# Up projections with 512-column matmuls over both operand parts, and new prices in the planner of an encoder kernel

## The chip, the core and the metric

One NeuronCore of a Trainium2 chip runs the whole program. TensorE (PE) multiplies, VectorE (DVE) and ScalarE (ACT) do the elementwise work, GpSimd (POOL) issues a few copies, SyncE (SP) issues nearly all loads. The metric is the device time of one execution in microseconds.

## What is computed

Two layers on x of 256 frames by 1024 channels, all in float32. Cut to what matters here:

```python
def swiglu_ffn(x, w_up, w_down):              # w_up: 1024 x 5632, w_down: 2816 x 1024
    a, b = jnp.split(x @ w_up, 2, axis=-1)
    return (jax.nn.silu(a) * b) @ w_down

for l in range(DEPTH):                        # DEPTH = 2
    x = x + 0.5 * swiglu_ffn(rmsnorm(x, ffn1_norm[l]), ffn1_w_up[l], ffn1_w_down[l])
    proj = rmsnorm(x, mix_norm[l]) @ w_in[l]  # 1024 x 5120
    # three branches on parts of proj: S5 state space model, chunked attention,
    # convolution module; each gated, summed, then one projection w_out
    x = x + merged @ w_out[l]
    x = x + 0.5 * swiglu_ffn(rmsnorm(x, ffn2_norm[l]), ffn2_w_up[l], ffn2_w_down[l])
```

## The kernel before

Activations are held transposed: 128 channels on the partitions, 256 frames along the free axis. So a weight tile is 128 x 128, stationary, and 256 columns of frames pass over it. To keep nearly float32 accuracy with the faster F32R matmul, each operand is split in two parts, `hi` and `lo` = value - `hi`, and a product is hi x hi + hi x lo + lo x hi.

Weights come from HBM in chunks of eight tiles (512 KB). For each chunk SP loads `raw` (3 buffers), ACT casts it to `hi` (4 buffers), DVE subtracts to get `lo` (4 buffers). A few small branch weights stay in float32 and are loaded straight into `lo` buffers. A norm's two parts of the operand lie side by side in one tile `x2` (128 x 8 x 2 x 256), in the profile `x`; the gated FFN activations lie the same way in a tile `a2`, in the profile `AB`.

`ffn` (four calls) has an up stage and a down stage. The up stage runs over 22 pairs of column blocks: block `i` gives the part through the silu, block `22 + i` the factor. Each block is 8 tiles, three matmuls of 256 columns each in `prod` (operands given as a tuple). Both halves of a pair share one PSUM bank of 512 columns, taken in turn from the rings `mm` (3 banks) and `at` (2). Then DVE multiplies the first half by `rb` (the norm's factor, spread over the partitions), ACT takes a tanh, DVE finishes the silu and multiplies by the second half from PSUM, ACT and DVE split the result into `AB`. The scratch tiles of this are the ring `ev` (4 buffers). The down stage runs over 8 column blocks of 22 tiles; `prod` gets its operand as one tile there, and passes both parts at once over a `hi` tile (512 columns, the hi x hi sum in the left half of the bank, hi x lo in the right) and the `hi` part over the `lo` tile (256 columns, left half). ACT copies the right half out, DVE adds the left.

The other PSUM rings are `pq`, `y` (S5 branch) and `ax` (norms, attention outputs, convolution norm), one bank each. A norm's end (`norm_end`) sums squares with four matmuls of one column (`ax<-ones,acc`), takes a reciprocal root on DVE, and spreads it by a slow float32 matmul (`ax<-sq,ones`) that ACT copies to `rb`. The convolution's layer norm in the mixer (`conv_norm`) ends in the same way: DVE makes `sq`, PE spreads it, ACT copies, DVE multiplies `cv` with it and goes on, and then `cv` feeds the branch matmuls `w_br_conv`. The `gh` tile of the S5 branch feeds `s5_w_glu` beside them.

The program is not written in the order in which it runs. A recorder takes every operation; `schedule` then plays a list scheduling with a price for each (`price`: how long it holds its engine, and the delay until its result counts), and the instructions are issued in the order found, each engine in order. Among ready operations the lowest rank goes first: -2 for a norm's end, 0 for the main line, 1 for the attention heads, 2 for the convolution, 3 for the S5 states, 4 for the S5 tables of a layer (given to `ffn1` as `fill`, made on DVE and ACT from scratch tiles `sa`, `sc`, `mc`, `bs` for use in that layer's mixer). All helper matmuls of ranks over 0 run as -1. Since every recorded operation is issued from one line, all have one line in the profile (L289); they are told apart by tiles.

Of the kernel before, what the change touches and what calls it, by code (L numbers as in the profile page):

```python
# [18 lines left out]
F32R = mybir.dt.float32r  # L19
I32 = mybir.dt.int32  # L20
AF = mybir.ActivationFunctionType
ALU = mybir.AluOpType
AX = mybir.AxisListType
PSUM = bass.MemoryType.PSUM

L, P, T, DM, DFF = 2, 128, 256, 1024, 2816
KD, KF = DM // P, DFF // P
# [99 lines left out]
class Recorder:  # L127
# [85 lines left out]
    @staticmethod  # L213
    def price(eng, name, outs, ins, kw):
        n = 1
        for d in list(outs[0].ap)[1:]:
            n *= d[1]
        if name == "dma_start":
            return (max(0.5, 1.43e-3 * n), 2.0) if eng == "sp" else (1.0, 2.0 + 2.5e-3 * n)
        if eng == "pe":  # L220
            if name == "transpose":
                return 0.112, 0.2
            slow = kw["rhs"].dtype != F32R or n < 256
            rows = outs[0].partition_size()
            return max(n / 2400.0 * (4 * rows / P if slow else 1) + 0.0025, 0.03), 0.2
        if eng == "act":
            return 0.12 + n / 1200.0 + (0.1 if kw.get("accum_out") is not None else 0), 0.2
        if name == "reciprocal":
            return 0.06 + 8 * n / 960.0, 0.16
        if name == "tensor_reduce":  # L230
            n = 1
            for d in list(ins[0].ap)[1:]:
                n *= d[1]
        fast = name in ("tensor_scalar", "tensor_copy") and all(a.space != PSUM for a in outs + ins)
        scal = 0.06 if any(a.free_size() == 1 for a in ins) and n > 1 else 0
        return SLACK * (0.068 + scal + n / (1920.0 if fast else 960.0)), 0.16

    def schedule(self):
        import heapq
# [52 lines left out]

X_LOADS = {(0, 0): (0, 1), (0, 512): (1, 2), (1, 0): (2, 4), (2, 0): (4, 8)}
MARGIN, AUX_MARGIN = 0.3, 0.8
SLACK = 1.02
WARM = 5
RAW = 3
RANKS = (1, 2, 3)
# [2 lines left out]
class Builder:  # L301
# [183 lines left out]
    def ffn(self, l, name, after=None, fill=()):  # L485
        nc = self.nc
        up, down = name + "_w_up", name + "_w_down"
        a2 = self.tile(self.big, [P, KF, 2, T], F32R, "AB")
        fill = list(fill)
        first = l == 0 and name == "ffn1"  # L490
        ops = (self.xh, self.xl)
        pq = []
        for i in range(KF):
            if i == 0 and first:
                pq = [self.bank(t)[:, :T] for t in ("mm", "mm", "mm", "at")]
                self.quad(pq, l, up, (0, KF, 1, KF + 1), ops, KD)
                self.norm_end()
            elif i == 0:
                pq = [self.bank()[:, :T] for _ in range(2)]
                self.pair(pq, l, up, (0, KF), ops, KD)  # L500
                self.norm_end()
            elif not pq:
                ps = self.bank(("mm", "mm", "mm", "at", "at")[(i + 1) % 5])
                pq = [ps[:, :T], ps[:, T:]]
                for o, c in zip(pq, (i, KF + i)):
                    self.block(o, l, up, c, ops, KD)
            rb = self.rb
            t = self.tmp("ev")
            nc.vector.tensor_tensor(out=t, in0=pq.pop(0), in1=rb, op=ALU.mult)
            th = self.tmp("th")  # L510
            nc.scalar.activation(out=th, in_=t, func=AF.Tanh, scale=0.5)
            nc.vector.scalar_tensor_tensor(out=t, in0=th, scalar=1.0, in1=t, op0=ALU.add, op1=ALU.mult)
            nc.vector.tensor_tensor(out=t, in0=t, in1=pq.pop(0), op=ALU.mult)
            nc.scalar.copy(out=a2[:, i, 0, :], in_=t)
            nc.vector.tensor_tensor(out=a2[:, i, 1, :], in0=t, in1=a2[:, i, 0, :].bitcast(F32), op=ALU.subtract)
            if i == 0:
                self.rank(4)
                for f in fill:
                    f()
                self.rank(0)  # L520
        if after is not None:
            self.norm_start(*after)

        def evac(j, ps):
            t = self.tmp("ev")
            nc.scalar.copy(out=t, in_=ps[:, T:])
            nc.vector.tensor_tensor(out=t, in0=ps[:, :T], in1=t, op=ALU.add)
            nc.vector.scalar_tensor_tensor(out=t, in0=t, scalar=0.25, in1=rb, op0=ALU.mult, op1=ALU.mult)
            nc.vector.tensor_tensor(out=self.x[:, j, :], in0=self.x[:, j, :], in1=t, op=ALU.add)
            if after is not None:  # L530
                self.norm_block(j)
            else:
                nc.sync.dma_start(out=self.out_d[:, j, :], in_=self.x[:, j, :])

        p2 = [self.bank(), self.bank()]
        self.pair(p2, l, down, (0, 1), a2, KF)
        for j in range(KD):
            ps = p2[j] if j < 2 else self.bank()
            if j >= 2:
                self.block(ps, l, down, j, a2, KF)  # L540
            evac(j, ps)
# [584 lines left out]
```

## Time and profile before

| | us |
|---|---|
| median of 3 runs (1165.84 to 1168.61) | 1166.5 |
| the profiled execution | 1166.6 |
| its span, first to last instruction | 1164.8 |
| PE matmul busy in it | 1151.6 |
| DVE busy | 924.8 |
| ACT busy | 643.9 |

The span is what the trace covers; the execution's own time is 1.8 us more. The stages can be found by what PE reads: `x` in the up stages and `w_in`, `AB` in the down stages, `cv`, `u` and `gh` in the branch projections, `tbl` in `w_out`. In the order of time: up stage 4.7 to 136.7 us, down stage to 198.9, mixer of layer 0 to 397.5, up to 525.0, down to 586.9, then layer 1 in the same way from 586.9. "Idle before" is the time that an engine stood still ahead of an instruction, with what ended it. A matmul's duration (0.28 us for 256 columns) holds its way through the array; the next one starts after some 0.12, so pitches are read from starts.

### The profile page before, as it was taken

Reading aid. Unit: us, or ns where it says so; the run is one execution under the profiler, and the core shown is the slowest. Engines: PE = TensorE matmul, PEld = TensorE weight load, DVE = VectorE, ACT = ScalarE, POOL = GpSimd, SP = SyncE. Lnnn points to the kernel's source line nnn. Section 1 sums busy time; section 2 is a strip of 40 time slices with the busy share of each in tenths; the row PEclk is TensorE's granted clock in tenths of the full one; section 3 lists DMA queues with packets and bytes.
Section 4 is the critical chain, followed back from the end, with each engine's and each line's share of the span. In section 5 each row is a group of like instructions: output and inputs, shape, how many; then the busy total and the mean of one; then the engine's idle time right before and its main releaser. Section 6 shows DMA issues by size and latency. Waiting matters only on the chain.

```text
span 1164.8 us, 21936 instructions
## 1 busy us (share of the span) xinstructions
PE 1151.6 (99%) x8565; PEld 1086.8 (93%) x8565; DVE 924.8 (79%) x1898; ACT 643.9 (55%) x1171; POOL 13.0 (1%) x32
## 2 busy tenths in 40 slices
PE   8999999999998999999999999999999999999998
PEld 7999988889997999998899999898999999999987
DVE  7999976899998888766676666769999897666654
ACT  7546654797662556544544444547876535444442
POOL 0000000000200000000000000000001000000000
PEclk9999999999999999999999999999999999999999
DMA  7655556654542665555555555566554436555562
GB/s 258 216 182 182 191 184 217 199 194 152 172 153 93 182 198 181 192 184 186 184 178 184 184 187 188 183 217 200 180 166 157 145 125 191 187 184 183 181 200 89
DMA packets 59751, 209.97 MB, mean 180 GB/s; under 512 B 6912, under 2 KB 9088, under 8 KB 59392
## 3 DMA queue, kind: packets, MB, share of 16 engines
q1 hardware_dynamic: 58496, 207.79, 54.7%
q8 instruction: 67, 1.10, 0.4%
q0 software_dynamic: 1152, 0.79, 0.3%
q14 instruction: 36, 0.29, 0.1%
HBM read 206.72 MB, written 1.05 MB: 178 GB/s over the span
## 4 chain that ended last, share of the span: by engine, by line
PE 97%; DVE 1%; DMA 1%; ACT 1%; issue 0%; SPq 0%; ACTq 0%; DVEq 0%
PE mm L289 73%; PE at L289 21%; PE ax L289 1%; DMA raw<-in_w 1%; PE y L289 1%; PE pq L289 0%; DVE cv L289 0%; ACT hi L289 0%; DVE ev L289 0%; DVE lo L289 0%; ACT sq L289 0%; ACT x L289 0%; DVE bs L289 0%; SPq L289 0%; DVE sc L289 0%
## 5 line engine op out<-in xcount | busy, mean ns | idle before, releaser
L289 ACT CAST hi<-raw 128x1024 fp32r<-128x1024 f32 (+1 forms) x373 | 390.0, 1047 | 397.4 <-PE mm L289 189.3
L289 DVE TENSOR_TENSOR lo<-raw,hi 128x1024 fp32r<-128x1024 f32 (+1 forms) x373 | 454.7, 1221 | 157.1 <-ACT hi L289 153.9
L289 PE MATMUL mm<-x,hi 128*128 128x256 f32 x2736 | 502.0, 283 | 1.4 <-ACT hi L289 1.3
L289 PEld LDWEIGHTS mm<-x,hi 128*128 128x128 f32 x2736 | 423.8, 189 | 5.8 <-ACT hi L289 2.7
L289 PE MATMUL mm<-x,lo 128*128 128x256 f32 x1368 | 386.8, 284 | 0.3 <-DVE lo L289 0.2
L289 PEld LDWEIGHTS mm<-x,lo 128*128 128x128 f32 x1368 | 257.0, 188 | 1.9 <-DVE lo L289 0.7
L289 PE MATMUL mm<-AB,hi 128*128 128x512 f32 x704 | 246.6, 398 | 0.0
L289 PE MATMUL mm<-AB,lo 128*128 128x256 f32 x704 | 193.1, 281 | 0.0
L289 PE MATMUL at<-x,hi 128*128 128x256 f32 x1040 | 188.6, 282 | 0.6 <-ACT AB L289 0.6
L289 PEld LDWEIGHTS at<-x,hi 128*128 128x128 f32 x1040 | 160.6, 189 | 0.8 <-ACT AB L289 0.8
L289 PEld LDWEIGHTS mm<-AB,hi 128*128 128x128 f32 x704 | 130.6, 188 | 29.7
L289 PE MATMUL at<-x,lo 128*128 128x256 f32 x520 | 146.5, 282 | 0.0
L289 PEld LDWEIGHTS mm<-AB,lo 128*128 128x128 f32 x704 | 132.9, 189 | 2.6
L289 PEld LDWEIGHTS at<-x,lo 128*128 128x128 f32 x520 | 97.8, 188 | 0.0
L289 PE MATMUL mm<-tbl,hi 128*128 128x256 f32 x256 | 46.5, 284 | 0.0
L289 PE MATMUL at<-hi,x 128*128 128x512 f32 x128 | 41.0, 396 | 0.0
L289 PEld LDWEIGHTS mm<-tbl,hi 128*128 128x128 f32 x256 | 40.1, 192 | 0.1
L289 ACT ACTIVATE th<-ev 128x256 f32<-128x256 f32 x88 | 36.2, 412 | 7.0 <-DVE ev L289 6.9
L289 ACT CAST AB<-ev 128x256 fp32r<-128x256 f32 x88 | 35.0, 400 | 6.7 <-DVE ev L289 6.4
L289 DVE SCALAR_TENSOR_TENSOR ev<-th,ev 128x256 f32<-128x256 f32 x88 | 36.8, 419 | 1.2 <-ACT th L289 1.2
L289 DVE TENSOR_TENSOR AB<-ev,AB 128x256 fp32r<-128x256 f32 x88 | 36.6, 419 | 0.8 <-ACT AB L289 0.7
L289 DVE TENSOR_TENSOR ev<-mm,rb 128x256 f32<-128x256 f32 x56 | 23.6, 423 | 15.8 <-PE mm L289 12.9
(222 smaller groups left out, 1136.1 us busy)
## 6 DMA issues: line engine op xcount, KB each, us to landing
raw<-in_w SPq DMA_DIRECT2D x371, 512.0 KB, 4.2
lo<-in_w SPq DMA_DIRECT2D x10, 512.0 KB, 3.7
AB<-in_b SPq DMA_DIRECT2D x2, 1536.0 KB, 7.3
mc<-in_s SPq DMA_DIRECT2D x8, 192.0 KB, 4.5
out_x<-px SPq DMA_DIRECT2D x8, 128.0 KB, 2.8
raw<-in_w SPq DMA_DIRECT2D x2, 256.0 KB, 3.8
px<-in_x SPq DMA_DIRECT2D x1, 512.0 KB, 6.7
ct<-in_p SPq DMA_DIRECT2D x2, 256.0 KB, 4.0
```

The source lines that it names most:

```text
L289: fn(*args, **kw)
```

## The change

1. In `ffn` the up blocks get the operand as the one tile `x2`. `prod` then does for them what it does in the down stage: `hi` tile under 512 columns, `lo` tile under 256, left and right half of a bank of their own. So a pair of blocks takes two banks; they come in turn from `mm` x3, `at` x2, `pq`, `y`.
2. When a block leaves PSUM, ACT copies the right half to an `ev` tile, DVE adds the left half to it. The multiply by `rb` and the one by the second block read these. A pair takes two `ev` tiles instead of one; the ring keeps its 4 buffers.
3. `price` gets other numbers: 0.120 us for an F32R matmul of 256 columns (was 0.109), 0.235 for 512 (was 0.216), 4-pass matmuls and matmuls of one column apart, ACT operations with a per-partition scalar 0.06 dearer, the DVE factor `SLACK` = 1.02 gone, the scan at half the rate, DVE with an accumulator 0.06 dearer.

```diff
@@ price
-                return 0.112, 0.2
-            slow = kw["rhs"].dtype != F32R or n < 256
-            rows = outs[0].partition_size()
-            return max(n / 2400.0 * (4 * rows / P if slow else 1) + 0.0025, 0.03), 0.2
+                return 0.1, 0.2
+            if n == 1:
+                return 0.224, 0.2
+            if kw["rhs"].dtype != F32R or n < 256:
+                rows = outs[0].partition_size()
+                return max(n / 2370.0 * 4 * rows / P, 0.03), 0.2
+            return n / 2240.0 + 0.006, 0.2
...
-        return SLACK * (0.068 + scal + n / (1920.0 if fast else 960.0)), 0.16
+        rate = 1920.0 if fast else 480.0 if name == "tensor_tensor_scan" else 960.0
+        return 0.068 + scal + n / rate + (0.06 if kw.get("accum_out") is not None else 0), 0.16
@@ ffn
-        ops = (self.xh, self.xl)
+        turn = iter(("mm", "mm", "mm", "at", "at", "pq", "y") * KF)
...
             elif not pq:
-                ps = self.bank(("mm", "mm", "mm", "at", "at")[(i + 1) % 5])
-                pq = [ps[:, :T], ps[:, T:]]
+                pq = [self.bank(next(turn)) for _ in range(2)]
                 for o, c in zip(pq, (i, KF + i)):
-                    self.block(o, l, up, c, ops, KD)
+                    self.block(o, l, up, c, self.x2, KD)
             rb = self.rb
-            t = self.tmp("ev")
-            nc.vector.tensor_tensor(out=t, in0=pq.pop(0), in1=rb, op=ALU.mult)
+            t, u = self.tmp("ev"), self.tmp("ev")
+            for v in (t, u):
+                ps = pq.pop(0)
+                nc.scalar.copy(out=v, in_=ps[:, T:])
+                nc.vector.tensor_tensor(out=v, in0=ps[:, :T], in1=v, op=ALU.add)
+            nc.vector.tensor_tensor(out=t, in0=t, in1=rb, op=ALU.mult)
...
-            nc.vector.tensor_tensor(out=t, in0=t, in1=pq.pop(0), op=ALU.mult)
+            nc.vector.tensor_tensor(out=t, in0=t, in1=u, op=ALU.mult)
```

How the instructions stand, before and after. PE inside an up stage, a few tiles of one block (`x` is the operand, `hi` and `lo` the weight chunk; x2 marks two matmuls in a row). Before:

```order
L289 MATMUL at_342<-x_15_108,hi_335 128x256 x2
L289 MATMUL at_342<-x_15_108,lo_336 128x256
L289 MATMUL at_342<-x_15_108,hi_335 128x256 x2
L289 MATMUL at_342<-x_15_108,lo_336 128x256
L289 MATMUL at_342<-x_15_108,hi_335 128x256 x2
```

and after:

```order
L294 MATMUL mm_376<-x_15_108,hi_368 128x512
L294 MATMUL mm_376<-x_15_108,lo_369 128x256
L294 MATMUL mm_376<-x_15_108,hi_368 128x512
L294 MATMUL mm_376<-x_15_108,lo_369 128x256
L294 MATMUL mm_376<-x_15_108,hi_368 128x512
```

Two matmuls of 256 columns have become one of 512, and the bank is the block's own. From the third pair on, every block's 16 matmuls stand in one piece in all four up stages.

DVE in the mixer of layer 0, at the end of the convolution's norm: from `sq`, which PE spreads, to the operations that finish `cv` (`bs`, `sc`, `sa` belong to the S5 tables of layer 1, `AB_549` to the attention branch's output). Before:

```order
L289 TENSOR_SCALAR sq_668<-ident,y_572_665 128x128 x2
L289 TENSOR_TENSOR bs_1233<-mc_1236,bs_1233 32x512
L289 TENSOR_TENSOR bs_1233<-mc_1237,bs_1233 32x512
L289 TENSOR_SCALAR sc_1260<-iota,f_1256 128x256
L289 TENSOR_SCALAR sa_1262<-iota,fh_1257 128x256
L289 SCALAR_TENSOR_TENSOR sa_1259<-sc_1260,sa_1259 128x256
L289 TENSOR_SCALAR sc_1263<-iota,f_1256 128x256
L289 TENSOR_SCALAR sc_1266<-iota,f_1256 128x256
L289 TENSOR_TENSOR cv_561<-cv_561,cv_667 128x256 x2
L289 SCALAR_TENSOR_TENSOR sa_1262<-sc_1263,sa_1262 128x256
L289 TENSOR_SCALAR cv_672<-cv_561,px 128x256
```

and after:

```order
L294 TENSOR_SCALAR sq_710<-ident,y_614_707 128x128 x2
L294 SCALAR_TENSOR_TENSOR AB_549<-AB_549,mm_866 128x256
L294 SCALAR_TENSOR_TENSOR AB_549<-AB_549,mm_868 128x256
L294 TENSOR_TENSOR cv_603<-cv_603,cv_709 128x256 x2
L294 TENSOR_SCALAR cv_714<-cv_603,px 128x256
L294 SCALAR_TENSOR_TENSOR cv_603<-cv_713,cv_714 128x256
```

The seven table operations have moved to earlier places; two that read the last attention blocks from PSUM stand there now.

PE in the first up stage, where the first four blocks end and the norm is spread (`ax`). `hi_97` is the fourth chunk, `hi_122` the fifth, `hi_125` the sixth. Before:

```order
L289 MATMUL mm_117<-x_15_108,hi_97 128x256
L289 MATMUL mm_118<-x_15_108,hi_97 128x256
L289 MATMUL mm_119<-x_15_108,hi_97 128x256
L289 MATMUL at_120<-x_15_108,hi_97 128x256
L289 MATMUL at_198<-x_15_108,hi_122 128x256 x2
L289 MATMUL ax_133<-sq_132,ones 128x256
```

and after:

```order
L294 MATMUL at_200<-x_15_108,hi_122 128x512
L294 MATMUL pq_201<-x_15_108,hi_125 128x512
L294 MATMUL ax_133<-sq_132,ones 128x256
L294 MATMUL mm_117<-x_15_108,hi_97 128x512
L294 MATMUL mm_118<-x_15_108,hi_97 128x512
L294 MATMUL mm_119<-x_15_108,hi_97 128x512
```

A matmul on the sixth chunk has moved ahead of the spread and of the last tiles of the first four blocks.

## Rows read from the trace of the kernel before

**Rows 1.** The page, parts 1 and 4: busy time of engines, and the chain.

```profile
PE 1151.6 (99%) x8565; PEld 1086.8 (93%) x8565; DVE 924.8 (79%) x1898; ACT 643.9 (55%) x1171; POOL 13.0 (1%) x32
...
PE 97%; DVE 1%; DMA 1%; ACT 1%; issue 0%; SPq 0%; ACTq 0%; DVEq 0%
```

**Rows 2.** Waits: who waited for whom, sum, times, longest.

```profile
ACT hi L289 <- PE mm L289: 189.3, 141, 4.1
...
PE mm L289 <- DVE cv L289: 4.0, 2, 3.5
```

**Rows 3.** Timeline of PE in an up stage: start, length, instruction.

```profile
99.90 0.28 PE L289 MATMUL mm<-x,lo 128*128 128x256 f32 x1
...
105.66 0.28 PE L289 MATMUL mm<-x,lo 128*128 128x256 f32 x1
```

**Rows 4.** Stretches (length; busy of PE, PEld, DVE, ACT, POOL; clock): up, down, up, down.

```profile
4.70:136.70 132.00, 129.78 (x1062) 128.69 (x1063) 119.85 (x307) 78.69 (x114) 0.34 (x1) 1.00 0.64 208
136.70:198.90 62.20, 62.20 (x354) 53.99 (x353) 45.92 (x103) 31.22 (x45) 0.00 (x0) 1.00 0.58 191
397.50:525.00 127.50, 127.50 (x1064) 127.45 (x1063) 103.86 (x211) 69.58 (x95) 0.00 (x0) 1.00 0.56 183
525.00:586.90 61.90, 61.90 (x354) 53.95 (x353) 41.15 (x60) 31.21 (x45) 0.00 (x0) 1.00 0.57 187
```

**Rows 5.** Groups of instructions by form: busy us, mean ns, idle before.

```profile
L289 DVE TENSOR_TENSOR lo<-raw,hi 128x1024 fp32r<-128x1024 f32 x371 | 453.4, 1224 | 156.2 <-ACT hi L289 152.9 <-PE mm L289 0.6
L289 ACT CAST hi<-raw 128x1024 fp32r<-128x1024 f32 x371 | 388.8, 1049 | 396.6 <-PE mm L289 189.3 <-issue 109.4 <-PE at L289 68.2
L289 ACT CAST AB<-ev 128x256 fp32r<-128x256 f32 x88 | 35.0, 400 | 6.7 <-DVE ev L289 6.4
L289 DVE SCALAR_TENSOR_TENSOR ev<-ev,rb 128x256 f32<-128x256 f32 x32 | 13.2, 423 | 0.8
L289 DVE TENSOR_TENSOR ev<-mm,ev 128x256 f32<-128x256 f32 x32 | 13.1, 420 | 16.5 <-ACT ev L289 16.5
L289 ACT COPY ev<-mm 128x256 f32<-128x256 f32 x32 | 11.8, 371 | 30.0 <-PE mm L289 29.5
```

**Rows 6.** Timeline of DVE: one pair's way to `AB`, and what follows what.

```profile
450.36 0.42 DVE L289 TENSOR_TENSOR ev<-at,rb 128x256 f32<-128x256 f32 x1
450.71 0.28 DVE L289 TENSOR_SCALAR tbl<-tbl 128x256 f32<-128x256 f32 x1
...
454.25 1.23 DVE L289 TENSOR_TENSOR lo<-raw,hi 128x1024 fp32r<-128x1024 f32 x1 [0.39 <-ACT hi L289]
455.39 0.42 DVE L289 TENSOR_TENSOR AB<-ev,AB 128x256 fp32r<-128x256 f32 x1
```

**Rows 7.** Timeline of PE before `cv`, layer 0 and layer 1.

```profile
352.60 0.59 PE L289 MATMUL ax<-sq,ones 128*128 128x256 f32 x2
...
357.11 0.70 PE L289 MATMUL mm<-cv,lo 128*128 128x256 f32 x2 [3.48 <-DVE cv L289]
...
928.73 0.60 PE L289 MATMUL ax<-sq,ones 128*128 128x256 f32 x2
...
931.61 0.70 PE L289 MATMUL mm<-cv,lo 128*128 128x256 f32 x2 [0.56 <-DVE cv L289]
```

**Rows 8.** Stretches: branch projections of layers 0 and 1; PE alone after the stop.

```profile
351.30:374.20 22.90, 19.42 (x83) 16.44 (x82) 19.53 (x53) 5.01 (x11) 0.00 (x0) 0.93 0.29 95
929.10:947.00 17.90, 17.34 (x81) 14.95 (x80) 15.73 (x41) 4.76 (x10) 0.00 (x0) 1.00 0.35 118
...
358.00:361.50 3.50, 3.50 (x11) 0.52 0.00 0
```

**Rows 9.** Timeline of PE and ACT in the first stage.

```profile
19.56 0.59 PE L289 MATMUL ax<-sq,ones 128*128 128x256 f32 x2
...
27.23 0.47 PE L289 MATMUL at<-x,hi 128*128 128x256 f32 x2 [0.61 <-ACT AB L289]
...
18.97 1.05 ACT L289 CAST hi<-raw 128x1024 fp32r<-128x1024 f32 x1 [0.61 <-DMA raw<-in_w]
```

More of the change, by code (lines that the diff above doesn't have):

```diff
@@ L221, in price @@
             if name == "transpose":
-                return 0.112, 0.2
-            slow = kw["rhs"].dtype != F32R or n < 256
-            rows = outs[0].partition_size()
-            return max(n / 2400.0 * (4 * rows / P if slow else 1) + 0.0025, 0.03), 0.2
+                return 0.1, 0.2
[5 more added lines that the diff above has]
+            return n / 2240.0 + 0.006, 0.2
+        scal = 0.06 if any(a.free_size() == 1 for a in ins) and n > 1 else 0
+        psum = any(a.space == PSUM for a in outs + ins)
         if eng == "act":
-            return 0.12 + n / 1200.0 + (0.1 if kw.get("accum_out") is not None else 0), 0.2
+            return 0.12 + n / 1200.0 + scal + (0.1 if kw.get("accum_out") is not None else 0), 0.2
         if name == "reciprocal":
@@ L233, in price @@
                 n *= d[1]
-        fast = name in ("tensor_scalar", "tensor_copy") and all(a.space != PSUM for a in outs + ins)
-        scal = 0.06 if any(a.free_size() == 1 for a in ins) and n > 1 else 0
-        return SLACK * (0.068 + scal + n / (1920.0 if fast else 960.0)), 0.16
+        fast = name in ("tensor_scalar", "tensor_copy") and not psum
+        rate = 1920.0 if fast else 480.0 if name == "tensor_tensor_scan" else 960.0
+        return 0.068 + scal + n / rate + (0.06 if kw.get("accum_out") is not None else 0), 0.16
     def schedule(self):
@@ L294 @@
 MARGIN, AUX_MARGIN = 0.3, 0.8
-SLACK = 1.02
 WARM = 5
@@ L494, in ffn @@
             if i == 0 and first:
-                pq = [self.bank(t)[:, :T] for t in ("mm", "mm", "mm", "at")]
-                self.quad(pq, l, up, (0, KF, 1, KF + 1), ops, KD)
+                pq = [self.bank(next(turn)) for _ in range(4)]
+                self.quad(pq, l, up, (0, KF, 1, KF + 1), self.x2, KD)
                 self.norm_end()
             elif i == 0:
-                pq = [self.bank()[:, :T] for _ in range(2)]
-                self.pair(pq, l, up, (0, KF), ops, KD)
+                pq = [self.bank(next(turn)) for _ in range(2)]
+                self.pair(pq, l, up, (0, KF), self.x2, KD)
                 self.norm_end()
             elif not pq:
-                ps = self.bank(("mm", "mm", "mm", "at", "at")[(i + 1) % 5])
-                pq = [ps[:, :T], ps[:, T:]]
+                pq = [self.bank(next(turn)) for _ in range(2)]
                 for o, c in zip(pq, (i, KF + i)):
-                    self.block(o, l, up, c, ops, KD)
+                    self.block(o, l, up, c, self.x2, KD)
             rb = self.rb
-            t = self.tmp("ev")
-            nc.vector.tensor_tensor(out=t, in0=pq.pop(0), in1=rb, op=ALU.mult)
+            t, u = self.tmp("ev"), self.tmp("ev")
[4 more added lines that the diff above has]
+            nc.vector.tensor_tensor(out=t, in0=t, in1=rb, op=ALU.mult)
             th = self.tmp("th")
```

## The prediction, made before the run

> **What bounds the kernel now.** I read the page's first two parts, then the waits, then each stage. TensorE's matmul row is busy for 1151.6 of 1164.8 us and the chain that ended last is 97% PE [rows 1]. A busy matmul row alone proves little, so I looked at the idle time: in the whole list of waits PE's longest sum is 4.0 us, for DVE's `cv`, two times [rows 2]. So nearly every microsecond of the span is spent in the pitch of the matmuls, and only two things can move it: a cheaper matmul stream, or the few places where PE stands still. VectorE (924.8 us) and ScalarE (643.9 us) have room on average [rows 1], but this change hands them work, so their room has to be read in the stages that get it.
>
> **The matmuls of the up projections.** There are four up stages (two layers, two FFNs) of 352 weight tiles each (44 column blocks by 8). Before, a tile costs three matmuls of 256 columns; now one of 512 and one of 256. The 768 columns stay, one of three matmuls and one of three weight loads go. In a clean stretch of an up stage the `lo` matmuls of two tiles that lie 16 tiles apart start at 99.90 and 105.66 [rows 3]: 5.76 us / 16 = 0.360 us for a tile of three.
>
> The new form has its exact twin in the down projections: one matmul of 512 over both parts, one of 256, 8 blocks of 22 tiles, 176 pairs in a stage. Those take 61.9 us in one stage and 62.2 in another [rows 4], with nothing else on PE: 0.352 to 0.353 us a pair. So a tile gets 0.007 to 0.008 us cheaper, 2.3 to 2.9 us in a stage. I take 2.6, and the stage of 127.5 us [rows 4] becomes one of 124.9. In the first stage the first 32 tiles are paced by loads and casts, which leaves 2.6 x 320/352 = 2.4. Sum: 3 x 2.6 + 2.4 = **10.2 us less**, bounds 9.0 to 11.5.
>
> The Trainium skill has a price of its own (TensorE: Matmul & The Clock Gate, section Wait — 56ns, not 53.3ns?): N columns at 2.4 GHz and some 2.5 ns for each matmul. By it 1408 matmuls fewer would save 3.5 us. The trace does not agree: 0.120 us for 256 columns in the three-matmul tile is 13 ns over 256/2.4, so more goes with a matmul than that.
>
> **The work that leaves PSUM.** Each of the 88 column pairs (22 in a stage) gets two copies on ScalarE and two adds on VectorE; the multiplies by `rb` and by the second half stay and read SBUF instead of PSUM. The same copy and add stand in the down stages: 0.371 us and 0.420 us [rows 5]. So 176 x 0.371 = 65 us more ScalarE and 176 x 0.420 = 74 us more VectorE, none of it on PE. The moved multiply costs nothing: 0.42 us from the PSUM bank `at` [rows 6], 0.423 us for one that reads `ev` and `rb` [rows 5].
>
> Does it stay hidden? Per column pair PE needs 16 x 0.352 = 5.6 us. VectorE has two weight splits of 1.224 and now six operations of 0.42: 4.97 us by durations. By start-to-start it is less: a split at 454.25 is followed at 455.39, a 256-wide operation at 450.36 is followed at 450.71 [rows 6], so 2 x 1.14 + 6 x 0.35 = 4.4 us, 78%. ScalarE: two casts of 1.049, two copies, a tanh and a cast of 0.40 [rows 5] = 3.6 us, 65%. Steady state holds. Only the first stage is over-full: VectorE is busy there for 119.85 of 132.0 us [rows 4] because the layer's S5 tables are made in its gaps, and 44 adds at 0.35 make 135.2, some 5 us more than the shorter stage has. The tables have the lowest rank, and the following down stage leaves 62.2 - 45.9 = 16.3 us of VectorE free [rows 4]; in the new order they do end there. I price this at 0.
>
> PSUM: a column pair held one bank of a ring of five, now it holds two of seven. That is 3.5 pairs or 19.7 us in flight against 28.8. The adds free a bank without waiting for `rb`, which the old multiply had to; I take 0.
>
> **The order of the mixer in layer 0.** The new prices re-plan everything. At the convolution's end PE stands for 3.48 us for `cv` (357.11), behind a spread at 352.60 [rows 7]. In layer 1 the same chain goes from 928.73 to 931.61, with 0.56 us of idle PE [rows 7]. The difference is VectorE's queue: in layer 0, between `sq` (which feeds the spread) and the multiply of `cv`, seven operations for the next layer's tables stand in the old order, and none in the new (the piece of the order above). After PE has stood there the granted clock falls: 0.52 in 358 to 361.5, nearly all of it at the lower level of 1.2 GHz, and 0.93 over the stage, against 1.00 in layer 1 [rows 8]. From the first `gh` to the first `tbl` matmul layer 0 takes 22.9 us, layer 1 17.9 us [rows 8], for the same matmuls. With layer 1's VectorE order I expect layer 1's time: **5.0 us less**. Upper bound 5.5 (the 0.56 goes too), lower bound 1 (another operation is late and the clock still falls).
>
> **The start.** PE waited 0.61 us at 27.23 for a bank of the ring `at` [rows 9]; the new rings free it. Against that, the new order puts the first matmul of the third pair's second block (`pq<-x`, on the chunk whose cast ran from 18.97 for 1.05 us [rows 9]) ahead of the spread, which PE reached at 19.56 [rows 9], so it waits there for some 0.6 us. Net 0, bounds -0.8 to +1.
>
> **The rest of the plan.** The planner used to think that a 256-column matmul takes 0.109 us where the trace shows 0.120. It placed helpers as if PE ran fast, so in reality they came early. With true prices that hidden slack goes. The trace of before does not show this; its nearest rows are layer 1's 0.56 us and layer 0's 3.48 us of waiting [rows 7]. I take +0.5, nearer to the small one since the planner still adds margins; bounds -1 to +4.
>
> **Sum.** The profiled execution took 1166.6 us (span 1164.8); the median of the runs is 1166.5, so the sum needs no shift. 1166.6 - 10.2 - 5.0 + 0 + 0.5 = 1151.9, say **1152 us**. All bounds the good way give 1147, all the bad way 1162; they won't all fall together.
>
> **Rivals.** *A, the pitch comes, the mixer does not:* the re-planned mixers of either layer get a wait of 2 to 5 us somewhere else (at heads, scores or branch blocks, where PE takes small matmuls between large ones). For it: the plan changes in hundreds of places and 97% of the chain hangs on PE. Against: the layer-0 stop has a plain cause that the new order lacks. 1166.6 - 10.2 - 1 + 3 = 1158.
>
> *B, slower: the scratch ring `ev` sets the pace.* It has four buffers; a column pair took one and now takes two, so two pairs are in flight instead of four. A pair's first buffer is held from its first copy to the end of the split into `AB`. Before, from the multiply at 450.36 to the split's end at 455.81, it was 5.4 us [rows 6], with two splits of `lo` and ScalarE's casts in between; now come the 2.8 us until the second bank is full: 8.3 us against 2 x 5.6 = 11.3. It decides from 11.3 us on, if every one of the four new steps queues behind one more 1.2 us split or cast. ScalarE waits 189.3 us in all for PE to free `hi` buffers, up to 4.1 us at a time [rows 2], and a copy behind such a cast waits too. At 13 us a pair's pace is 6.5 us, 0.9 over: 88 x 0.9 = 79 us, less 15: 1230. At 11.6 us it is 5.8, 0.17 over: 88 x 0.17 = 15 us, the whole gain: 1166. The Trainium skill (TensorE: Matmul & The Clock Gate, section Architectural detail) has ScalarE and VectorE as strict first-in first-out queues, which is what would make this happen; rows 2 agree that a cast holds its queue.
>
> *C, weight loads set the pace.* The load row is busy 127.45 of 127.5 us in the up stage for 1063 loads [rows 4], 0.120 each. If that were the limit, two loads would make a tile 0.240 us: 1408 x 0.12 = 169 us less, 998 us. Against it: the down stage has the same two loads for a pair, its load row is busy for only 53.95 of 61.9 us [rows 4], and the pair still takes 0.352. The Trainium skill (Perfetto Trace Analysis, Identifying the Most-Contended Engine) takes the busy share of weight loads, not of matmuls, as the measure of how near TensorE is to its limit; by it C would be the likely one. The down stage speaks against that reading here.
>
> *D, no gain:* the adds' and copies' traffic slows the 512-column stream in the up stages to the old 0.360, and the mixer finds a new stop: 1166. The down stages run such copies beside the stream without harm, but only eight of them in a stage.
>
> **How the numbers follow.** Forecast (1147 to 1156) 0.68; A (1156 to 1162) 0.20; B 0.06, of which 0.04 above 1170; C 0.01; D 0.05. The range 1146 to 1160 takes the forecast with its bounds and most of A. A measurement here tells 0.3% (3.5 us) from no change: faster than 1163: 0.68 + 0.20 + 0.01 + some of D and B = 0.92; same 0.04; slower 0.04.
>
> **What would show it.** Right: each up stage some 125 us from first `x` to first `AB` matmul, 0.352 us a tile; no idle PE at `cv` over 1 us in layer 0 and a granted clock of 1.00 from there to `w_out`; that stage near 18 us; VectorE's busy share in the up stages up by some 15 us each, PE waiting for it nowhere. Wrong: PE waiting for `ev` copies or adds (B), a new wait of over 2 us in a mixer (A), a tile at 0.360 (D) or far under 0.35 (C).

## The result, and the profile after

The changed kernel takes 1151.15 us (median of 4 runs, 1150.59 to 1152.70) against 1167.16 for the kernel before in the same series (1165.84 to 1168.61): a ratio of 0.9861, 95% interval 0.9847 to 0.9876, so 1.4% faster. The forecast was 1152.0, within 1146 to 1160. The profiled execution took 1151.5 us with a span of 1149.7, 15.1 less than before.

The page after, parts 1 and 4, to be read against [rows 1]:

```profile
PE 1137.6 (99%) x7157; PEld 1009.1 (88%) x7157; DVE 983.0 (86%) x2074; ACT 699.7 (61%) x1347; POOL 13.0 (1%) x32
...
PE 81%; DVE 14%; DMA 1%; ACT 1%; issue 1%; SPq 0%; DVEq 0%; ACTq 0%
```

PE has 1408 matmuls and 1408 weight loads fewer and is still busy all the time: the busy matmul row fell by 14.0 us while VectorE's rose by 58 and ScalarE's by 56 (58.2 / 176 = 0.33 us for each added add, near the start-to-start time of [rows 6] and not the length of 0.42; 0.32 for each copy). The chain that ended last now passes through VectorE for 14%, some 160 us: 97 of them in the first up stage, 58 in the two mixers, 5 in the first down stage, none in the other up stages. That isn't time that PE stands still. The chain goes back from each instruction to what released it last, so one short wait of PE sends it into VectorE's queue, and there it stays as long as that queue has no gap. What PE loses stands in its waits. All of them, with sum, times and the longest:

```profile
PE mm L1019 <- ACT iota L1015: 2.3, 1, 2.3
PE y L294 <- DVE lo L294: 1.1, 1, 1.1
PE mm L294 <- ACT hi L294: 1.1, 1, 1.1
PE mm L294 <- DVE lo L294: 1.0, 2, 0.8
PE mm L294 <- DVE cv L294: 0.9, 2, 0.4
PE pq L294 <- ACT hi L294: 0.4, 1, 0.4
PE pq L294 <- DVE sc L294: 0.3, 2, 0.2
PE mm L294 <- DVE x L294: 0.2, 1, 0.2
```

The 4.0 us for `cv` of [rows 2] are down to 0.9. New are 1.1 us for `lo` at a `y` matmul (a bank that up stages did not use before) and, of the 1.0 us for `lo` at `mm`, the 0.8 in the first down stage. So PE does wait for VectorE in the first two stages, where the forecast had it wait nowhere. The stages, from a window for each (length; busy PE, PEld, DVE, ACT, POOL; clock, DMA share, GB/s), in the order up, down, mixer, up, down of layer 0:

```profile
4.70:134.75 130.05, 126.93 (x711) 108.98 (x712) 124.03 (x315) 83.98 (x151) 0.35 (x1) 1.00 0.63 203
134.75:197.87 63.12, 62.33 (x354) 53.98 (x353) 53.31 (x142) 36.97 (x52) 0.00 (x0) 1.00 0.63 204
197.87:392.25 194.38, 193.78 (x1455) 179.38 (x1454) 181.20 (x411) 128.62 (x310) 6.01 (x12) 1.00 0.54 175
392.25:516.40 124.15, 124.15 (x710) 108.25 (x709) 116.60 (x255) 82.55 (x139) 0.00 (x0) 1.00 0.57 187
516.40:578.35 61.95, 61.95 (x354) 53.97 (x353) 41.13 (x60) 31.28 (x45) 0.00 (x0) 1.00 0.57 187
```

Against [rows 4] the second up stage is 3 us shorter, and its weight-load row is busy for 108 of 124 us where it was full. VectorE's busy time in it grew from 104 to 117.

For comparing kernels I count each stage by starts of matmuls alone. The first up stage begins with its first `x` matmul, every other stage where the one before it ends; an up stage ends with the first `AB` matmul behind it, a down stage with its last `AB` matmul, a mixer with its last `tbl` matmul. Counted so, in us of the profiled executions (E1 and E2 are the first two experiments below, E7 the seventh):

| stage | before | after | E1: new form, old prices | E2: old form, new prices | E7: old prices in the first stages |
|---|---|---|---|---|---|
| up 1 (layer 0, ffn1) | 132.08 | 129.90 | 128.05 | 134.30 | 127.93 |
| down 1 | 61.95 | 62.82 | 61.67 | 61.66 | 61.67 |
| mixer 0 | 198.66 | 194.31 | 198.65 | 194.29 | 194.98 |
| up 2 | 127.70 | 124.53 | 124.52 | 127.70 | 124.53 |
| up 3 | 127.80 | 124.61 | 124.61 | 127.81 | 124.61 |
| mixer 1 | 194.00 | 194.22 | 194.03 | 194.01 | 194.56 |
| up 4 | 127.70 | 124.53 | 124.53 | 127.70 | 124.53 |
| span | 1164.8 | 1149.7 | 1151.0 | 1163.1 | 1147.6 |

The other three down stages stay between 61.66 and 61.95 in every column. The pitch itself, on a timeline of PE in up 2 (start, length, instruction), two matmuls 16 tiles apart:

```profile
412.91 0.39 PE L294 MATMUL mm<-x,hi 128*128 128x512 f32 x1
...
418.52 0.40 PE L294 MATMUL mm<-x,hi 128*128 128x512 f32 x1
```

5.61 us / 16 = 0.351 us a tile, where [rows 3] gave 0.360. And the place of the old stop, PE's timeline before `cv` in layers 0 and 1, against [rows 7]:

```profile
350.33 0.60 PE L294 MATMUL ax<-sq,ones 128*128 128x256 f32 x2
...
351.00 1.89 PE L294 MATMUL mm<-gh,lo 128*128 128x256 f32 x8
353.32 0.70 PE L294 MATMUL mm<-cv,lo 128*128 128x256 f32 x2 [0.43 <-DVE cv L294]
...
918.72 0.70 PE L294 MATMUL mm<-cv,lo 128*128 128x256 f32 x2 [0.43 <-DVE cv L294]
```

The stop of 3.48 us is one of 0.43, and the stage behind it, first `gh` to first `tbl`, takes 17.8 us at a clock of 1.00 (22.9 at 0.93 in [rows 8]):

```profile
351.00:368.80 17.80, 17.36 (x83) 15.00 (x81) 15.91 (x41) 4.75 (x10) 0.00 (x0) 1.00 0.37 119
```

### The profile page after: what moved, and what is told of

Its sections match the earlier page's. It is cut to its first block, busy times and chain, and to the rows that moved or that the text cites. A ratio compares the mean times of both kernels' runs of the same rounds, so it can differ in the third digit from the quotient of the medians.

```text
span 1149.7 us, 19592 instructions
## 1 busy us (share of the span) xinstructions
PE 1137.6 (99%) x7157; PEld 1009.1 (88%) x7157; DVE 983.0 (86%) x2074; ACT 699.7 (61%) x1347; POOL 13.0 (1%) x32
## 4 chain that ended last, share of the span: by engine, by line
PE 81%; DVE 14%; DMA 1%; ACT 1%; issue 1%; SPq 0%; DVEq 0%; ACTq 0%
PE mm L294 57%; PE at L294 14%; DVE lo L294 6%; PE y L294 5%; PE pq L294 5%; DVE ev L294 3%; DVE cv L294 2%; DMA raw<-in_w 1%; PE ax L294 1%; DVE AB L294 1%; ACT hi L294 0%; DVE tbl L294 0%; ACT tbl L294 0%; DVE sc L294 0%; DVE sa L294 0%
## 5 line engine op out<-in xcount | busy, mean ns | idle before, releaser
L294 PE MATMUL mm<-x,hi 128*128 128x256 f32 (+1 forms) x1600 | 405.6, 330 | 1.4 <-ACT hi L294 1.1
L294 PE MATMUL mm<-x,lo 128*128 128x256 f32 x1120 | 302.7, 282 | 0.3 <-DVE lo L294 0.2
L294 PEld LDWEIGHTS mm<-x,hi 128*128 128x128 f32 x1600 | 266.9, 188 | 26.9 <-ACT hi L294 2.8
L294 PE MATMUL at<-x,hi 128*128 128x512 f32 x384 | 135.5, 394 | 0.0
L294 PEld LDWEIGHTS at<-x,hi 128*128 128x128 f32 x384 | 70.6, 188 | 13.0
L294 DVE TENSOR_TENSOR ev<-mm,ev 128x256 f32<-128x256 f32 x112 | 46.8, 422 | 29.4 <-ACT ev L294 29.3
L294 PE MATMUL pq<-x,hi 128*128 128x512 f32 x192 | 69.5, 394 | 0.4 <-ACT hi L294 0.4
L294 PE MATMUL y<-x,hi 128*128 128x512 f32 x192 | 69.4, 394 | 0.0
L294 PE MATMUL y<-x,lo 128*128 128x256 f32 x192 | 49.9, 280 | 1.1 <-DVE lo L294 1.1
L294 PE MATMUL pq<-x,lo 128*128 128x256 f32 x192 | 49.8, 280 | 0.0
```

What stands on the lines that cost most here:

```text
L294: fn(*args, **kw)
```

## The experiments

**E1 and E2: form and prices apart.** E1 is the changed kernel with the old `price` (and `SLACK`), E2 the kernel before with the new one.

```
E1:  def price(...):           # body of the kernel before
     SLACK = 1.02
E2:  def price(...):           # body of the changed kernel; SLACK gone
     ops = (self.xh, self.xl)  # up projections as before
```

> The new up projections with the old prices of the scheduler. Theory (the gain of the up stages is the matmul form, the gain in the mixer is the order that the new prices make): each of the last three up stages takes 124.2 us as in the changed kernel, 3.2 less than before; the seven table operations stand again between sq and the multiply of cv on VectorE in layer 0, so the stop of about 3.5 us and the fall of the clock behind it are back, and the mixer of layer 0 takes 198 to 199 us. Time 1166.5 - 11 = 1155 to 1157. Rival (the prices also give part of the gain in the up stages, by keeping PE fed): up stages of 125 to 127, time 1159 to 1163. Rival (the stop in the mixer went because the up stages got shorter): mixer near 194.4, time 1151.

> The old up projections (three matmuls of 256 columns) with the new prices. Theory: up stages as before, 127.4 to 127.5 us each; no table operation between sq and the multiply of cv in layer 0, so a wait under 1 us there, clock 1.00, mixer of layer 0 near 194.4 us; time 1166.5 - 4 to 5 = 1161 to 1163. Rival (the new form causes the mixer's gain): mixer 198.7, time 1166. With the run of the new form under old prices the two gains should add up to that of the changed kernel, about 15.5 us, within 1.5 us.

Measured: E1 1151.79 us (1150.53 to 1153.57; ratio 0.9867, 0.9849 to 0.9884), E2 1164.54 (1161.14 to 1166.70; ratio 0.9977, 0.9968 to 0.9987). The table shows a clean split. The last three up stages are 3.2 us shorter with the new form whatever the prices, and unchanged with the old form. Mixer 0 is 4.35 us shorter with the new prices whatever the form. In E1 the same seven table operations stand again on VectorE between `sq` and the multiply of `cv`, in E2 none; in E1 the stop is back, and so is the low clock behind it (PE's waits, then a window with the clock behind ACT's and POOL's columns):

```profile
PE mm L289 <- DVE cv L289: 4.0, 2, 3.5
...
353.00:357.00 4.00, 3.63 (x10) 3.02 (x11) 1.33 (x4) 0.87 (x2) 0.00 (x0) 0.59 0.00 0
```

So both mechanisms stand as predicted, and neither needs the other. But the times missed the expectations. E2 was expected at 1161 to 1163 and took 1164.5. E1 was expected at 1155 to 1157 and came in at 1151.8, nearly the changed kernel's time: that the new prices gain anything in the whole time, on top of the new form, isn't shown. The prices' 4.35 us in mixer 0 are mostly given back in the first two stages. With either form the first up stage is longer under the new prices (132.08 to 134.30, and 128.05 to 129.90), and in the new form the first down stage is too (61.67 to 62.82). By spans the form alone is worth 13.8 us, the prices alone 1.7, and both 15.1; by medians 15.2, 2.4 and 16.0. Part of E2's 134.30 is chance: its profiled execution has a stop of 1.92 us for `hi` at 28.16, with a low clock behind it (length, busy PE, clock, DMA share, GB/s):

```profile
29.10:32.50 3.40, 3.40 (x19) 0.50 0.25 76
```

Over the whole profiled execution the granted clock is 0.998. In seven of E2's ten executions it is 1.000, which leaves no place for such a stretch.

**E3: the sines behind the last pair.** The 1.0 us for `lo` at `mm` lies in the first down stage. PE's timeline there, and then ScalarE's, in the changed kernel:

```profile
144.35 0.39 PE L294 MATMUL mm<-AB,lo 128*128 128x256 f32 x1 [0.79 <-DVE lo L294]
```

```profile
135.80 1.05 ACT L294 CAST hi<-raw 128x1024 fp32r<-128x1024 f32 x1
136.87 1.28 ACT L294 ACT_TABLE_LOAD   x1
138.16 1.92 ACT L294 ACTIVATE tbl<-tbl 128x2048 f32<-128x2048 f32 x1
139.99 0.34 ACT L294 COPY ev<-mm 128x256 f32<-128x256 f32 x1
140.35 1.28 ACT L294 ACT_TABLE_LOAD   x1
141.64 0.42 ACT L294 ACTIVATE th<-ev 128x256 f32<-128x256 f32 x1
141.97 1.03 ACT L294 CAST hi<-raw 128x1024 fp32r<-128x1024 f32 x1
```

The second sine of layer 0's tables (`tbl<-tbl`) falls between the two copies of the last pair. The function table is loaded for the sine and loaded again for the pair's tanh, 1.28 us each, which no price contains. The Trainium skill (ScalarE: Activation LUTs, section What ACT_TABLE_LOAD costs) gives 1.28 us for the load and some 1.38 more for a drain with every switch; the load agrees, the drain isn't in these rows (the cast ends at 136.85, the load starts at 136.87, the sine 0.01 us after its end). From the end of one cast at 136.85 to the start of the next at 141.97 pass 5.1 us. In the kernel before, each of the two sines ran inside the up stage, with a load on either side, and PE waited for neither. E3 makes the sines follow the last pair:

```
-    rank 4: all of the table's steps, at the first pair
+    rank 4: all but the sines and what follows them, at the first pair
+    after the last pair: the sines, behind its last instruction; then the rest
```

> The changed kernel; only the two sine activations of layer 0's tables are put behind the last pair of the first up stage in ScalarE's queue. Theory (the 1.04 us that PE waits near 143 us comes from ScalarE, which changes its function table twice, 1.28 us each, around the second sine, between the copies and the tanh of the last pair, so that casts and splits come late): that wait goes or falls under 0.3 us, and the function table is changed once there instead of four times over the first two stages; time 0.5 to 1.5 us less, 1150. Rival (VectorE, full in the first stage, is simply behind): the wait stays at about 1 us, time the same within 0.5 us. Second rival: two sines in a row (3.7 us and a table change) delay a cast by themselves and a wait of 1 to 2 us comes at the new place.

Measured: 1150.83 us (1149.45 to 1152.89), and the first down stage at 61.67 us: the wait is gone. ScalarE's timeline of E3 shows one table load, both sines in a row and then three casts that PE doesn't wait for:

```profile
140.68 1.05 ACT L297 CAST hi<-raw 128x1024 fp32r<-128x1024 f32 x1
141.74 1.28 ACT L297 ACT_TABLE_LOAD   x1
143.04 3.72 ACT L297 ACTIVATE tbl<-tbl 128x2048 f32<-128x2048 f32 x2
146.66 2.94 ACT L297 CAST hi<-raw 128x1024 fp32r<-128x1024 f32 x3
```

So it is ScalarE's sequence that made PE wait. VectorE had no room to make it good: the chain of the changed kernel runs through its queue up to this sine. In E3, without this wait, VectorE's share of the chain is 5%:

```profile
PE 92%; DVE 5%; ACT 1%; DMA 1%; issue 1%; SPq 0%; DVEq 0%; ACTq 0%
```

The whole time didn't move, though: the mixers took 195.21 and 194.98 (0.9 and 0.8 more, with a wait of 0.5 us for `us` that the new plan made) and the first up stage 130.66. A change worth 1 us is lost in what re-planning does elsewhere.

**E4: what a stop costs.** PE's stop for `cv` is made again, in a kernel that has none.

```
     cv = cv * rl                       # two multiplies
+    for n in range(8 - 4 * l):         # change nothing
+        cv[n % 2] = max(cv[n % 2] * 1.0, cv[n % 2])
```

> The changed kernel; on VectorE, between the multiply of cv by its spread factor and the rest of that chain, eight operations of 256 columns that change nothing are added in layer 0 and four in layer 1 (0.34 us each start to start); PE's order is unchanged. It measures what a stop of PE at this place costs. Theory (a stop of about 3 us costs itself and then a stretch at the lower clock): layer 0's wait grows from 0.43 to about 3.1 us, the granted clock falls to about 0.5 for some 3 us behind it, and the mixer of layer 0 takes 4 to 5 us more than in the changed kernel. Layer 1's wait grows from about 0.5 to 1.8 us; if the clock holds there it costs 1.4 us, if it falls 3 us. Time 1156 to 1158.5. Rival (the clock's fall before had another cause, and a stop costs only itself): 2.7 + 1.4 = 4 us, 1155, clock 1.00 throughout.

Measured: 1155.67 us (1155.15 to 1155.96). In layer 0 PE stops for 2.99 us and the mixer takes 198.45, 4.14 more than in the changed kernel. A timeline row of PE, and the window behind the stop (length, busy PE, clock, DMA share, GB/s):

```profile
355.63 1.22 PE L294 MATMUL mm<-cv,lo 128*128 128x256 f32 x2 [2.99 <-DVE cv L294]
```

```profile
355.60:359.00 3.40, 3.37 (x8) 0.53 0.00 0
```

2.56 us of the 4.14 are the longer wait; the other 1.6 are the clock, at 0.53 for 3.4 us as in [rows 8] after the 3.48. In layer 1 the expectation failed: the planner put all eight `gh` matmuls in front of `cv` there instead of two, the wait stayed at 0.55 and the mixer at 194.37, and so the time lies a little under the 1156 to 1158.5 expected. What a stop of this length does to the clock can be read elsewhere, and it goes both ways. In E8 (below) PE stops for 1.24 us at 911.29, in layer 1's attention heads, and works at half the clock behind it; in E9 it stops for 1.78 us at 214.30, and the granted clock stays at 1.00. The stretch behind E8's stop:

```profile
912.55:915.95 3.40, 3.40 (x33) 0.50 0.00 0
```

**E5 and E6: the scratch ring** (rival B). One number each.

```
-TMP = dict(ev=4, ...
+TMP = dict(ev=3, ...        (E5)      ev=2   (E6)
```

> The changed kernel with three buffers in the scratch ring ev instead of four. In the changed kernel's trace a pair holds its first buffer from its first copy to the end of the split for 5.8 us (643.94 to 649.72), not the 8.3 that the prediction worked out; with three buffers the second copy of the next pair, 8.4 us after the first of this one, needs it. Theory (hold 5.8 us): the up stages stay at 124.5 to 124.6 us, time within 1.5 us of the changed kernel. Rival (hold of 8.3 us and more, as predicted): the ring is on the edge, up stages grow by 1 us and more each.

> The changed kernel with two buffers in ev: a pair can't copy its first block before the split of the pair before is done. Theory (hold 5.8 us, and some 0.2 us from one engine to the next): a pair every 6.0 us instead of 5.61, the last three up stages 130 to 133 us, the first, where VectorE is full, 10 to 30 us longer, time 1151 + 30 to 60 = 1180 to 1210. Rival (hold of 8.3 us): a pair every 8.5 us, 187 us a stage, time near 1400. Either way it shows that the ring is what the pair's chain hangs on once it is too small.

Measured: E5 1150.24 us, up stages 2 to 4 unchanged at 124.53 to 124.61. E6 1198.42 us (one execution each), but not evenly: up 1 146.32, up 2 130.14, up 3 and up 4 still 124.61 and 124.53, and the down stages of layer 0 10 and 12 us longer (72.50 and 73.23). In each of those two PE stops twice for 2.8 to 3.0 us for the last pairs' `AB`, and the granted clock is 0.50 for 6.8 us behind that. The hold can be read on ScalarE's and VectorE's timelines. In the changed kernel, the copy that opens a pair, its tanh, the copy of its second block, and the split that ends it:

```profile
643.94 0.37 ACT L294 COPY ev<-mm 128x256 f32<-128x256 f32 x1 [1.02 <-PE mm L294]
...
645.27 0.42 ACT L294 ACTIVATE th<-ev 128x256 f32<-128x256 f32 x1
646.80 0.37 ACT L294 COPY ev<-mm 128x256 f32<-128x256 f32 x1 [1.12 <-PE mm L294]
```

```profile
649.30 0.42 DVE L294 TENSOR_TENSOR AB<-ev,AB 128x256 fp32r<-128x256 f32 x1
```

643.94 to 649.72 is 5.8 us. In E6's up 4 the copy that opens a pair, the next pair's, and the split between them:

```profile
1043.08 0.38 ACT L294 COPY ev<-at 128x256 f32<-128x256 f32 x1 [1.06 <-DVE AB L294]
...
1048.69 0.37 ACT L294 COPY ev<-pq 128x256 f32<-128x256 f32 x1 [1.05 <-DVE AB L294]
```

```profile
1048.23 0.42 DVE L294 TENSOR_TENSOR AB<-ev,AB 128x256 fp32r<-128x256 f32 x1
```

The copy now waits for the split of the pair before and the chain tightens to 5.57 us, which is just inside PE's 5.61, and PE doesn't wait. In up 1 and up 2, where tables share VectorE, the chain is longer and PE waits for `ev`. So three buffers cost nothing here, and two are enough only where no tables are made. E6's expected range of 1180 to 1210 held, by its first stages; that up 3 and up 4 would be untouched wasn't expected.

**E7 and E12: old prices for the first stages only.** Every operation recorded before the first mixer is planned with the old prices, the rest with the new. E11 is the changed kernel again beside E12, which is E7 again.

```
-    cost, op.lat = self.price(...)
+    cost, op.lat = (self.old_price if self.early else self.price)(...)
+    self.nc.early = False          # ahead of the first mixer
```

> The changed kernel, but everything that is recorded before the first mixer (first up and down stage and the tables of layer 0) is planned with the old prices, the rest with the new ones. Theory (the new prices gain 4.35 us in the mixer of layer 0 and lose 1.9 us in the first up stage and 1.1 us in the first down stage): first up stage 128.0 and first down stage 61.7 as in the run of the new form under old prices, mixer of layer 0 at 194.3 as in the changed kernel, span 1151.0 - 4.35 = 1146.7, time 1147 to 1148.5, faster than both. Rival (the first stage's difference is chance from when the first transfers land): first stage 128 to 130, time 1149 to 1151.

> The changed kernel once more, timed next to the kernel with old prices in the first stage. Theory: 1151 us again; a first up stage of 129 to 130.5 us and a first down stage of 62.8 (with the wait of 1 us near 143 us), since both hang on the order of instructions and not on chance; the part before the spread moves by some 0.5 us with the first transfers.

> The changed kernel with the old prices for everything before the first mixer, once more, next to the changed kernel. Theory: first up stage 128 and first down stage 61.7 again, the mixers within 1 us of the changed kernel's, so 1.5 to 2.5 us faster than it in the same call. Rival (the difference of 1.2 us between their medians is within the spread of single runs, about 3 us): no difference over 1 us.

Measured: E7 1149.94 us (1148.52 to 1151.75), E12 1150.03 (1148.95 to 1150.66), E11 1150.36 (1150.16 to 1151.53). The first stages did what the theory says: up 1 127.93 and down 1 61.67 in both, against 128.93 and 62.97 in E11; PE waits for no `lo` over 0.2 us in E12. But mixer 0 took 194.98 and 195.13, 0.7 to 1.0 more than the changed kernel's. By spans it is 1147.6 and 1147.2 against 1149.7 and 1148.4; by the medians of E12 and E11, timed side by side, 0.3 us. So E7 missed its 1147 to 1148.5, and E12 its 1.5 to 2.5 us: E12's rival, no difference over 1 us, stands. A version that is faster than the changed kernel isn't shown. The first up stage of the changed kernel also moves by itself: 129.90 in one profile and 128.93 in another, where the wait at the first `y` is 0.2 us and not 1.1. So of the 1.9 us between it and E1, about half may be chance.

**E8: the form in the gate blocks.** On top of E7.

```
-    self.block(ps[:, :T], l, "w_in", G0 + b, ops, KD)
-    act(out=gth[:, b, :], in_=ps[:, :T], func=AF.Tanh, ...)
+    self.block(ps, l, "w_in", G0 + b, self.x2, KD)
+    ev = copy(ps[:, T:]);  ev = ps[:, :T] + ev
+    act(out=gth[:, b, :], in_=ev, func=AF.Tanh, ...)
```

> The kernel with old prices for the first stage, and the 24 gate blocks of each mixer also pass both parts of their operand at once (512 columns), with a copy on ScalarE and an add on VectorE on leaving PSUM: 24 x 8 = 192 tiles in a layer. Theory (the gain of the form is 0.009 us a tile wherever it is used, 3.2 us for 352 tiles): 1.7 us less in each mixer, 3.5 in all, time 1144 to 1145, if VectorE, busy for 181 and 176 of 194 us in the mixers, can take 24 x 0.35 = 8.4 us more in each. Rival (VectorE has no room there: its convolution and state chains end up to 8 us later, and PE waits for cv, u or tables): mixers 195 to 202 us, time 1148 to 1160.

Measured: 1160.23 us (1159.10 to 1162.23), 10 more than E7. Mixer 0 takes 204.77, mixer 1 196.93, against the rival's 195 to 202. Two of PE's waits in E8, a row of ScalarE ahead of the first of them, and the window of mixer 0:

```profile
PE at L320 <- ACT s L320: 4.2, 2, 2.9
...
PE mm L320 <- DVE cv L320: 2.3, 2, 1.9
```

```profile
335.50 0.40 ACT L320 ACTIVATE s<-s,mx 128x128 f32<-128x128 f32 x1 [2.69 <-DVE mx L320]
```

```profile
190.90:395.20 204.30, 196.42 (x1247) 169.44 (x1246) 190.80 (x462) 136.16 (x332) 5.99 (x12) 0.98 0.53 165
```

PE waits for the softmax's `s` from ScalarE, and for `cv`. ScalarE isn't the cause: it is busy for only 136 of 204 us, and it has itself stood for 2.69 us for `mx` of VectorE, whose queue is busy without a gap for the 10 us before. So the rival is right that VectorE has no room there. Behind two of PE's stops in mixer 0 (2.91 us for `s` and 1.11 for `nat`) the granted clock is 0.50 for 3.4 us each, 0.98 over the mixer. The copies and adds of the gates, of rank 0, also go ahead of the heads' and the convolution's operations of rank 1 and 2; how much is that order and how much VectorE's load (190.8 of 204.3) wasn't separated.

**E9 and E10: how much room VectorE has.** Two and six more operations of 256 columns in each pair's chain.

```
     t = t * u
+    for _ in range(2):             (E10: 6)
+        t = max(t * 1.0, t)
```

> The changed kernel with two more operations of 256 columns on VectorE for each column pair, on the pair's chain, which change nothing. Theory (VectorE stays hidden as long as a pair's start-to-start sum is under 5.61 us: two splits of 1.14 and now eight operations of 0.34 make 5.0): the last two up stages stay at 124.5 to 124.6 us, the second (with tables of layer 1 in it) within 1 us of that; the first, where VectorE has no idle time already, and the stages behind it that get its tables, lose 1 to 8 us; time 1152 to 1160. Rival (a queue at 89% already holds PE up in every stage): up stages of 126 and more, time above 1160.

> As before, with six more operations for each pair: 2 x 1.14 + 12 x 0.34 = 6.36 us against 5.61 of matmuls. Theory (start-to-start durations set the limit): the last two up stages become 22 x 6.36 = 140 us, 15 to 16 more each, the other two at least as much more, time 1151 + 65 to 100 = 1215 to 1250. Rival (the full lengths, 1.22 and 0.42, count, as the busy column suggests): 7.5 us a pair, 165 us a stage, time above 1310.

Measured (one execution each): E9 1158.39 us, with up 2 to up 4 at 124.63, 124.61 and 124.53: eight operations a pair still cost PE nothing. The loss of 7 us is in the first up stage (131.68) and above all in mixer 0 (199.50). Windows of E9's up 1, down 1 and mixer 0:

```profile
4.96:136.64 131.68, 127.93 (x711) 109.11 (x712) 125.17 (x311) 81.10 (x150) 0.14 (x1) 1.00 0.63 200
136.64:198.31 61.67, 61.67 (x353) 53.73 (x352) 61.47 (x178) 35.76 (x51) 0.00 (x0) 1.00 0.63 196
198.31:397.81 199.50, 194.80 (x1455) 179.46 (x1454) 184.12 (x421) 130.22 (x311) 5.99 (x12) 1.00 0.54 173
```

VectorE is busy for 61.47 of 61.67 us in down 1, so the tables that didn't fit into up 1 filled it; the last operations for S5 tables end at 201.5, in the mixer. PE then waits for `x`, `u` and `us`, 3.9 us in all, in the mixer's first 22 us. That the backlog of VectorE is the whole of mixer 0's loss isn't shown. E10 took 1222.48 us. Its up 4 and the down stage behind it take 134.87 + 67.77 instead of 124.53 + 61.67: 16.4 us for 22 pairs, 0.75 a pair, as 6.36 - 5.61 says. The 140 us expected for the up stage by itself didn't come: 6.1 of the 16.4 us fall into the down stage. Ten of the added operations in a row on VectorE's timeline of E10, and PE's longest sum of waits:

```profile
1066.46 3.43 DVE L294 SCALAR_TENSOR_TENSOR ev<-ev 128x256 f32<-128x256 f32 x10
```

```profile
PE mm L294 <- DVE lo L294: 15.3, 23, 1.3
```

(3.43 - 0.41) / 9 = 0.336 us from start to start, where the length is 0.41. The limit goes by the former: by lengths E9's pair would already need 2 x 1.22 + 8 x 0.42 = 5.8 us, over PE's 5.61, and E9's last up stages lose nothing.

## Why the prediction was right, point by point

**The pitch: right in kind, sized too small.** Forecast 2.6 us a stage (2.3 to 2.9), measured 3.17, 3.19 and 3.17. The term was mis-sized because unlike readings were set against each other: the old tile at 0.360 us, between two matmuls in a clean stretch [rows 3], the new one from whole down stages of 61.9 and 62.2 us, whose windows [rows 4] hold some 0.2 us of edges (counted by starts, 61.67 and 61.95). Like against like it is 0.009 us either way: 127.70 / 352 = 0.363 before and 124.53 / 352 = 0.354 after for whole stages, 0.360 and 0.351 between two matmuls. Whether the matmul or the weight load that goes with it is what saves the 0.009 us wasn't separated. Rival D (0.360 kept) and C (weight loads set the pace; 0.240 a tile) are out: 0.351 measured.

**The stop in mixer 0: right.** Forecast -5.0 for the stage behind `cv`, measured 22.9 to 17.8, with the order on VectorE as its cause (E1 and E2) and the clock as more than a third of its price (1.6 of 4.1 us in E4). Over the whole mixer it is -4.35; 0.75 was lost again elsewhere in it. **Rival A** is out: the new waits in the mixers are two of 0.2 us at `pq`.

**The first stage: 0 for the start was too kind.** The form alone gains 4.0 us there (E1; 2.4 forecast), and the new prices take 0.9 to 1.9 of it back. The wait of the first `pq` matmul ahead of the spread came as worked out (0.4 us in one profile, 1.0 in another, for 0.6).

**The tables at the end of the first stage: the wrong step.** They were priced at 0 because VectorE has 16 us free in the down stage. But the step that moved over the stage's end has a sine on ScalarE, and the two table loads of 1.28 us around it weren't in the working. Against the 61.67 us of E3 they cost 1.15 us in the profile, and 1.3 in E11's. A moved step has to be followed on every engine that it uses.

**The rest of the plan:** +0.5 forecast; mixer 1 +0.2, the first down stage +0.9, the other down stages together -0.3.

**Hidden work:** right. Start-to-start durations give the load of VectorE's queue; E9 and E10 bracket the limit between 5.0 and 6.4 us a pair, with PE's 5.61 in between. **Rival B** was priced on a chain of 8.3 us. The trace has 5.8: the 2.8 us until the second bank is full run beside the add, the multiply and the tanh of the first (643.94 to 646.80 in the rows of E5), and aren't added to the old chain. Its threshold (2 pairs, 11.2 us) is far off; with two buffers, not four, it came true where tables share VectorE (E6).

**Sum.** -10.2, -5.0, 0 and +0.5 were forecast. Measured by the table: up stages -11.7, mixer 0 -4.35, mixer 1, down stages and the edges +1.0; -15.1 in all. The terms missed by up to 1.5 us, in opposite directions. Set out by cause, the misses are larger: by the spans the form alone gave 13.8 us, where the pitch was to give 10.2, and the new prices on top of it 1.3, where 4.5 were forecast (5.0 less 0.5). That 1151.15 came so near to 1152.0 is in part these two cancelling out, and so luck. (All bounds the good way add up to 1148 and not 1147; nothing hangs on it.)

## What to carry to other kernels

Where TensorE is busy throughout, fewer and wider matmuls are worth their count only in nanoseconds a tile (0.009 us of 0.363 here), and the price is paid in evacuation work; ask of each stage by start-to-start times whether the other queues have room (4.4 and 5.0 of 5.61 us hidden, 6.36 not), since the same form lost 10 us in the mixers. Better prices for a planner are not better in every stage: here they removed a stop in one place and gave up to 3 us back in another, and two runs, form alone and prices alone, showed it stage by stage where the one total didn't. After any re-planning read the ends of stages: there the odd steps (a table load, a sine) land in someone's way.

## What was not expected of the hardware

- In the new tile the next matmul starts 0.232 us after one of 512 columns and 0.118 us after one of 256 (medians; together 0.350); in the old tile the three follow each other at 0.118 to 0.121 us (means; 0.361 in all). At the granted clock of 1.00 there, the level of 2.4 GHz, the 768 columns alone are 0.320 us. So three matmuls cost 0.041 us over their columns and two still cost 0.030: the wide one saves less than the mean 0.014 of a matmul.
- A function table load takes 1.28 us on ScalarE, and a sine between two tanh costs two of them.
- PE's clock fell to about half (0.53, for 3.4 us) after a stop of 2.99 us and of 3.48, and stayed at 1.00 after stops of 0.4 to 0.6 us at the same place. In other places it fell behind a stop of 1.24 us (E8) and didn't behind one of 1.78 (E9).
